# Low halves of split weights made by an accumulating DMA instead of VectorE, with a fourth weight tile pair, in a two-layer parallel-branch block

## The chip, the core and the metric

The kernel runs on one core of a Trainium2 chip. The metric is the device time of one execution in microseconds (us). The engines are TensorE (PE in the profile, with its weight loads shown as PEld), VectorE (DVE), ScalarE (ACT), GpSimd (POOL) and SyncE (SP), which here only issues DMA transfers. Each engine works through its own instructions in program order and waits on semaphores for the others.

## The reference, cut to what matters

Two layers act on a sequence x of 512 tokens and a context ctx of 256 tokens, both 1024 wide. In each layer a stream is normalised, scaled and shifted, and multiplied by a wide input matrix; four branches (retention, short convolution, a 31-tap convolution, attention) follow; each branch is multiplied by its own matrix and by a gate, and the sum goes through an output matrix.

```
hx = modulate(rmsnorm(x, norm_w[l]), shift_x, scale_x)
px = split_proj(hx @ w_in[l])               # q, k, v, gates of four branches
r, s, f, a = retention, short_conv, conformer_conv, windowed attention of px
merged = sum(sigmoid(g_i) * (br_i @ w_branch[i]) for i in range(4))
x = x + gate_x * (merged @ w_out[l])        # the context stream likewise in layer 0
```

All data are 32-bit floats.

## The kernel before

**Three products for one.** To keep 32-bit accuracy, each operand of a large matrix product is split in two float32r parts, a high part (the value copied to float32r) and a low part (the value minus its high part). The function `mm3` sums three products in PSUM: high weight by high data, high weight by low data, low weight by high data. A weight here is a block of 128 by 1024 numbers, eight 128 by 128 pieces, so one weight is 24 matmuls: of 512 columns for stream x, of 256 columns for the context.

**The path of a weight.** The list `wq` holds the weights in the order of their use. `w_load` takes the next one and issues its load on SP. A weight of stream x or of the output matrices of stream x is loaded whole (512 KB) into one of two raw tiles `w0`, `w1`. A weight of the context stream (its key ends in 1, called small below, since its product has 256 columns) is loaded in two halves of 256 KB into rows of the arena. `w_split` then makes the parts: ACT copies the raw data to the high tile `wh`, and DVE subtracts the high tile from the raw data into the low tile `wl` (lines 457 and 458). There are three pairs of tiles, `self.wt`, used in turn. `w_get` hands a weight to its matmuls, and `w_ahead(2)` splits until two weights beyond the one in use are ready. A gate weight ("g") brings along a block of 128 by 512 of a branch matrix, whose parts lie in arena rows; the change leaves those alone.

**What sets the order.** PE's instructions stand in the order in which the program is written. That order is made by `Tally`, a small planner: it adds up a cost for every instruction as it is issued, and `slot()` lets side work (attention, retention, the convolution, norms, written as generators) step forward between weights whenever the planner thinks that its inputs are ready and that DVE and ACT are not too far behind (`LEAD`, `LEADA`). Where side work waits for another engine's result, `settled()` adds `MARGIN`, 2 us, to the time at which the planner expects it. The other engines' orders are set by the framework's scheduler. Small powers of the norms run on POOL (`s_rs`, `s_rsr`, `s_lrs`).

**The stages.** Context of layer 0 (c0, small weights), stream x of layer 0 (x0), ten small weights for keys and values of the context in layer 1 (c1), stream x of layer 1 (x1). `final` computes the last output product in two halves of 256 columns, eight weights in the first half; three of them stay for the second half and five are loaded and split again.

All instructions are recorded through `call` of `Tallied`, so the profile puts nearly all of them on line 187; groups are told apart by tile names (`d`: PSUM of the large products; `k`: PSUM of side work; `p`: attention weights; `r`: arena rows).

Of the kernel before, what the change touches and what calls it, by code (L numbers as in the profile page):

```python
# [8 lines left out]
F32 = mybir.dt.float32  # L9
F32R = mybir.dt.float32r  # L10
BF16 = mybir.dt.bfloat16
AF = mybir.ActivationFunctionType
ALU = mybir.AluOpType
# [12 lines left out]
P = 128  # L26
# [97 lines left out]
class Row:  # L124
# [3 lines left out]
    def __init__(self, free, ring, tile, w, parts):  # L128
        self.free, self.ring = free, ring
        self.r = tile[:, :w] if parts else None  # L130
        self.a = tile[:, :w].bitcast(F32) if parts else tile[:, :w]
# [59 lines left out]
class Tally:  # L191
# [14 lines left out]
    def add(self, eng, op, a, k):  # L206
        aps = [x for x in (*a, *k.values()) if hasattr(x, "free_size")]
        out, src = aps[0], aps[1] if len(aps) > 1 else aps[0]
        n = src.free_size()
        ready = max([self.now, self.read.get(out.tensor.name, 0.0)] + [self.written.get(x.tensor.name, 0.0) for x in aps])  # L210
        if eng == "tensor":
            if op == "transpose":
                d = 0.109
            elif aps[2].dtype == F32:
                d = max(0.218, aps[2].free_size() / 600)
            else:
                d = aps[2].free_size() / 2400
                if aps[2].dtype == F32R and d < 0.1:
                    d = 0.213
            self.now += d  # L220
            end = self.now + 0.15
        else:
            if eng == "vector":
                d = 0.065 + n / 960
                if op in ("tensor_scalar", "tensor_copy") and n == src.free_size() and "PSUM" not in str(src.space):
                    d = 0.065 + n / 1920
            elif eng == "scalar":
                d = 0.1 + n / 1200
            elif eng == "gpsimd":
                d = 0.3 + n / 440  # L230
            else:
                d = 0.65
            start = max(self.busy[eng], ready)
            self.busy[eng] = max(self.busy[eng], self.now) + d
            end = start + d + 0.15
            if eng == "sync":
                end += 2.0 + n * out.shape[0] / 90000
        for x in aps:
            d = self.written if x is out or x is k.get("accum_out") else self.read
            d[x.tensor.name] = max(end, d.get(x.tensor.name, 0.0))  # L240
        self.last = max(self.last, end)
# [36 lines left out]
class Block:  # L278
    def __init__(self, ctx, tc, xc, vec, cst, w_a, w_g, w_b, w_o, w_m, out, out2):
        self.tc, self.nc = tc, Tally(tc.nc)  # L280
        self.xc, self.out, self.out2 = xc, out, out2
        self.wsrc = {"a": w_a, "g": w_g, "b": w_b, "o": w_o}
        self.w_m = w_m

        rp = ctx.enter_context(tc.tile_pool(name="rp", bufs=1))
        rp.tile([P, PAD], F32, name="fill")
        self.arena = Arena(rp, NROWS, 12)
        self.arena.relief = self.relief

        self.cp = cp = ctx.enter_context(tc.tile_pool(name="cp", bufs=1))  # L290
        self.wraw = [cp.tile([P, 1024], F32, name=f"w{i}") for i in range(2)]
        self.wt = [[cp.tile([P, 1024], F32R, name=f"w{p}{i}") for p in "hl"] for i in range(3)]
        self.pt = [cp.tile([P, 640], F32, name=f"p{i}") for i in range(6)]
        pp = ctx.enter_context(tc.tile_pool(name="pp", bufs=1, space=PSUM))
        nc = self.nc
        self.cst = cp.tile([P, NC_], F32, name="cst")
        self.vec = cp.tile([P, NV], F32, name="vec")
        nc.sync.dma_start(self.vec, vec)
        nc.sync.dma_start(self.cst[:, :NCE], cst[:, :NCE])
        self.late_consts = lambda: nc.sync.dma_start(self.cst[:, NCE:], cst[:, NCE:])  # L300
        self.rings = {}
        self.dense = [pp.tile([P, 512], F32, name=f"d{i}") for i in range(3)]
        self.ovs = [pp.tile([P, 512], F32, name="ov")]
        self.work = [pp.tile([P, 512], F32, name=f"k{i}") for i in range(4)]
        self.turn = {}
        self.wq, self.wraws, self.wready, self.wkeep = [], [], {}, {}
        self.lanes = [[] for _ in range(5)]
        self.turns = 0
        self.flow = None
# [115 lines left out]
    def w_load(self):  # L425
        key = self.wq.pop(0)
        kind, l, i, small = key
        nc = self.nc
        src = self.wsrc[kind][l, i]
        if small:  # L430
            raws = [(self.row(), slice(o, o + 512)) for o in (0, 512)]
            for r, o in raws:
                nc.sync.dma_start(r.a, src[:, o])
            raws = [(r, r.a, o) for r, o in raws]
        else:
            raw = self.take("wraw")
            nc.sync.dma_start(raw, src)
            raws = [(None, raw, slice(0, 1024))]
        if kind == "g":
            r = self.row()  # L440
            nc.sync.dma_start(r.a, self.wsrc["b"][l, i])
            raws.append((r, r.a, None))
        self.wraws.append((key, raws))

    def w_split(self):
        nc = self.nc
        key, raws = self.wraws.pop(0)
        parts = [self.take("wt")]
        for _, raw, o in raws:
            if o is None:  # L450
                hi, lo = self.part(), self.part()
                self.wkeep[key] = (hi, lo)
                hi, lo = hi.r, lo.r
                parts.append((hi, lo))
            else:
                hi, lo = (x[:, o] for x in parts[0])
            nc.scalar.activation(hi, raw, AF.Copy)
            nc.vector.tensor_tensor(lo, raw, hi.bitcast(F32), op=ALU.subtract)
        self.wready[key] = parts

    def w_ahead(self, n=2):
        while len(self.wready) < n and self.wraws:
            self.w_split()
        while self.wq and len(self.wraws) < (2 if self.wq[0][3] else 1):
            self.w_load()
# [1044 lines left out]
```

## Time and profile before

| quantity | value |
|---|---|
| median of 3 runs | 1831.37 us (1830.43 to 1831.96) |
| the profiled execution | 1828.66 us, of which the span from first to last instruction is 1826.9 us |
| granted TensorE clock, mean | 0.997 |
| busy share PE, PEld, DVE, ACT, POOL | 98%, 86%, 73%, 47%, 2% |
| DMA, all queues | 232.60 MB, mean 127 GB/s |

The span is what the trace shows; 1.8 us of the profiled execution lie around it. An engine's busy share is an average over stages that differ: what an engine's time is worth has to be read stage by stage, from what PE waits for there.

### The profile page before, as it was taken

To read this page: it belongs to the slowest core of one execution; us is meant where nothing else is said; L and a number is where in the kernel's file an instruction comes from. 1 tells how busy PE (TensorE), PEld (TensorE's weight loads), DVE (VectorE), ACT (ScalarE), POOL (GpSimd) and SP (SyncE) were. 2 spreads that over 40 slices of the span, in tenths; PEclk is the share of its full clock that TensorE was granted. 3 is DMA by queue.
4 is the path that set the end of the run, shared out by engine and by line. 5 is a ranking of instruction groups with operands and counts; after the bars stand their busy time and mean duration, and the time that the engine had idled before them with its cause. 6 is when DMAs were issued, how large, how long until landed. Compare 5 with 4: busy or idle time off the path is not lost. (4 is left out here: it accounts for less than half of the span.)

```text
span 1826.9 us, 27582 instructions
## 1 busy us (share of the span) xinstructions
PE 1798.4 (98%) x10242; PEld 1562.3 (86%) x10242; DVE 1326.9 (73%) x2635; ACT 851.6 (47%) x1625; POOL 27.9 (2%) x34
## 2 busy tenths in 40 slices
PE   6999999999999999999999999999999999999998
PEld 4999999988888888888888889888888888888888
DVE  8899999884556669996998457447999866344445
ACT  6666765553554544423423246445534554323223
POOL 1000000000000000000000000000000000000000
PEclk9999999999999999999999999999999999999999
DMA  9646477743222222233555552322222232332233
GB/s 315 246 129 207 120 239 231 233 138 116 70 70 68 83 81 80 95 113 124 183 167 170 159 190 76 116 70 70 65 92 84 84 95 91 111 105 90 87 116 116
DMA packets 104135, 232.60 MB, mean 127 GB/s; under 512 B 12864, under 2 KB 19776, under 8 KB 104000
## 3 DMA queue, kind: packets, MB, share of 16 engines
q1 hardware_dynamic: 104000, 230.84, 39.1%
q8 instruction: 80, 1.31, 0.3%
q14 instruction: 55, 0.45, 0.1%
HBM read 218.73 MB, written 5.24 MB: 123 GB/s over the span
## 5 line engine op out<-in xcount | busy, mean ns | idle before, releaser
L187 PE MATMUL d<-r,wh 128*128 128x512 f32 (+1 forms) x3136 | 942.8, 383 | 0.3 <-DVE r L187 0.3
L187 PEld LDWEIGHTS d<-r,wh 128*128 128x128 f32 x3136 | 572.7, 188 | 106.2 <-DVE r L187 0.8
L187 PE MATMUL d<-r,wl 128*128 128x512 f32 (+1 forms) x1568 | 597.6, 381 | 0.0
L187 DVE TENSOR_TENSOR wl<-w,wh 128x1024 fp32r<-128x1024 f32 x193 | 235.8, 1222 | 234.7 <-ACT wh L187 228.8
L187 ACT ACTIVATE wh<-w 128x1024 fp32r<-128x1024 f32 x193 | 204.9, 1062 | 412.0 <-PE d L187 354.8
L187 PEld LDWEIGHTS d<-r,wl 128*128 128x128 f32 x1568 | 294.8, 188 | 57.8
L187 ACT ACTIVATE r<-r 128x512 fp32r<-128x512 f32 (+3 forms) x264 | 150.6, 588 | 206.6 <-DVE r L187 93.8
L187 DVE TENSOR_TENSOR r<-r,r 128x512 fp32r<-128x512 f32 (+5 forms) x337 | 207.6, 630 | 33.4 <-ACT r L187 29.5
L187 DVE SCALAR_TENSOR_TENSOR r<-r,h_cfw,r 128x503 f32<-128x503 f32 (+19 forms) x360 | 229.4, 649 | 2.0
L187 PE MATMUL d<-r,r 128*128 128x512 f32 x768 | 184.8, 389 | 0.5 <-DVE r L187 0.5
L187 ACT ACTIVATE wh<-r 128x512 fp32r<-128x512 f32 x208 | 129.2, 630 | 101.7 <-PE d L187 90.0
L187 PEld LDWEIGHTS d<-r,r 128*128 128x128 f32 x768 | 144.1, 188 | 30.8 <-DVE r L187 0.9
L187 DVE TENSOR_TENSOR wl<-r,wh 128x512 fp32r<-128x512 f32 x208 | 140.6, 685 | 18.6 <-ACT wh L187 17.6
L187 DVE SCALAR_TENSOR_TENSOR r<-r,d 128x512 f32<-128x512 f32 (+1 forms) x156 | 92.8, 595 | 55.1 <-PE d L187 32.4
L187 ACT ACTIVATE r<-d 128x512 f32<-128x512 f32 (+2 forms) x234 | 118.5, 507 | 14.1 <-PE d L187 9.5
L187 PE MATMUL k<-r,r 128*128 128x128 f32 (+2 forms) x752 | 112.3, 290 | 2.7 <-ACT p L187 2.6
L187 ACT ACTIVATE r<-k 128x512 fp32r<-128x512 f32 (+4 forms) x162 | 77.0, 523 | 70.2 <-PE k L187 68.7
L187 PEld LDWEIGHTS k<-r,r 128*128 128x128 f32 x752 | 99.5, 191 | 9.0 <-ACT p L187 6.2
L187 ACT ACTIVATE p<-k,s_nm 128x256 f32<-128x256 f32 (+1 forms) x144 | 69.7, 496 | 77.0 <-DVE s_nm L187 76.8
L187 DVE SCALAR_TENSOR_TENSOR r<-r,cs,r 128x256 f32<-128x256 f32 x196 | 83.8, 480 | 1.0 <-DMA r<-w_m 0.4
L187 DVE TENSOR_TENSOR r<-k,r 128x512 fp32r<-128x512 f32 (+2 forms) x88 | 54.5, 653 | 9.2 <-ACT r L187 9.0
L187 ACT ACTIVATE p<-p,s_rc 128x512 f32<-128x512 f32 (+2 forms) x80 | 51.3, 719 | 8.6 <-DVE s_rc L187 8.6
(400 smaller groups left out, 2249.0 us busy)
## 6 DMA issues: line engine op xcount, KB each, us to landing
w<-w_a SPq DMA_DIRECT2D x108, 512.0 KB, 3.5
r<-w_a SPq DMA_DIRECT2D x128, 256.0 KB, 4.8
w<-w_g SPq DMA_DIRECT2D x64, 512.0 KB, 3.5
r<-w_m SPq DMA_DIRECT2D x96, 256.0 KB, 3.8
r<-w_b SPq DMA_DIRECT2D x96, 256.0 KB, 3.3
r<-w_g SPq DMA_DIRECT2D x64, 256.0 KB, 3.7
w<-w_o SPq DMA_DIRECT2D x21, 512.0 KB, 3.5
r<-xc SPq DMA_DIRECT2D x24, 256.0 KB, 3.9
```

The lines of the kernel that those rows point to most:

```text
L187: return f(*a, **k)
```

## The change

The low part of most weights is no longer made by DVE. ACT copies the high tile with factor -1 into the low tile, and a DMA that POOL issues then adds the weight, read once more from DRAM, to what stands there. This holds for every weight loaded whole after the third split, and for every other small weight (those whose running number is odd), there once for each half. There is a fourth pair of weight tiles, and `w_ahead` splits up to three weights ahead. The planner gets a cost for POOL's DMA, 1.0 us to issue and the landing time that it used for SP's.

```
             elif eng == "scalar":
                 d = 0.1 + n / 1200
+            elif eng == "gpsimd" and op == "dma_start":
+                d = 1.0
             elif eng == "gpsimd":
                 d = 0.3 + n / 440
...
-            if eng == "sync":
+            if op == "dma_start":
                 end += 2.0 + n * out.shape[0] / 90000
...
-        self.wt = [[cp.tile([P, 1024], F32R, name=f"w{p}{i}") for p in "hl"] for i in range(3)]
+        self.wt = [[cp.tile([P, 1024], F32R, name=f"w{p}{i}") for p in "hl"] for i in range(4)]
...
+        self.nsplit = 0
...
-            raws = [(r, r.a, o) for r, o in raws]
+            raws = [(r, r.a, o, src[:, o]) for r, o in raws]
         else:
             raw = self.take("wraw")
             nc.sync.dma_start(raw, src)
-            raws = [(None, raw, slice(0, 1024))]
+            raws = [(None, raw, slice(0, 1024), src)]
...
     def w_split(self):
         nc = self.nc
         key, raws = self.wraws.pop(0)
         parts = [self.take("wt")]
-        for _, raw, o in raws:
+        self.nsplit += 1
+        for _, raw, o, src in raws:
...
             nc.scalar.activation(hi, raw, AF.Copy)
-            nc.vector.tensor_tensor(lo, raw, hi.bitcast(F32), op=ALU.subtract)
+            if o and self.nsplit > 3 and (not key[3] or self.nsplit % 2):
+
+                nc.scalar.activation(lo, hi.bitcast(F32), AF.Copy, scale=-1.0)
+                nc.gpsimd.dma_start(lo, src, accum_op=ALU.add)
+            else:
+                nc.vector.tensor_tensor(lo, raw, hi.bitcast(F32), op=ALU.subtract)
         self.wready[key] = parts

-    def w_ahead(self, n=2):
+    def w_ahead(self, n=3):
```

In the built program 193 whole weights and 50 small ones go the new way. DVE loses 193 subtractions of 128x1024 and 100 of 128x512 (108 of that size stay), ACT gains as many copies `wl<-wh`, and POOL gains 293 DMA issues. PE has the same 9,700 rows of instructions in both programs; side work stands at other places among them.

DVE, in the attention of stream x, layer 1, where the largest scores (`s_mc`, `s_mx`) become the bias `s_nm` of the exponentials. Before:

```order
L187 TENSOR_REDUCE s_mx0_6125<-k0_160 128x1
L187 TENSOR_SCALAR s_ve3_2547<-s_mv3_2542 128x4
L187 TENSOR_REDUCE s_mx0_6125<-k1_161 128x1
L187 SCALAR_TENSOR_TENSOR r1414_13423<-r1361_12797,h_cfw1_763,r1414_13423 128x509
L187 TENSOR_TENSOR s_mc0_1876<-s_mc0_1876,s_mx0_6125 128x2
L187 TENSOR_TENSOR wl1_140<-w1_136,wh1_139 128x1024
L187 SCALAR_TENSOR_TENSOR s_nm0_1874<-s_mc0_1876,h_nsink1_769 128x2
L187 SCALAR_TENSOR_TENSOR r1414_13423<-r1361_12797,h_cfw1_763,r1414_13423 128x510
```

And with the change:

```order
L187 TENSOR_REDUCE s_mx0_6262<-k1_163 128x1
L187 TENSOR_REDUCE s_mx0_6262<-k2_164 128x1
L187 SCALAR_TENSOR_TENSOR r1390_13414<-r1361_13031,h_cfw1_765,r1390_13414 128x498
L187 TENSOR_TENSOR s_mc0_1939<-s_mc0_1939,s_mx0_6262 128x2
L187 SCALAR_TENSOR_TENSOR r1420_13773<-r1376_13247,h_cfw1_765,r1420_13773 128x503
L187 SCALAR_TENSOR_TENSOR s_nm0_1937<-s_mc0_1939,h_nsink1_771 128x2
L187 SCALAR_TENSOR_TENSOR r1390_13414<-r1361_13031,h_cfw1_765,r1390_13414 128x497
L187 SCALAR_TENSOR_TENSOR r1420_13773<-r1376_13247,h_cfw1_765,r1420_13773 128x504
```

Between the maximum `s_mc` and the bias `s_nm`, where the subtraction `wl` of a whole weight stood, a tap of the convolution stands now.

ACT, the same softmax: the copies of the splits and the exponentials `p`. Before:

```order
L187 ACTIVATE wh1_139<-w1_136 128x1024
L187 ACTIVATE r1419_13533<-d2_158 128x512
L187 ACTIVATE p4_147,s_ac0_1875<-k0_160,s_nm0_1874 128x256
L187 ACTIVATE p4_147,s_ac0_1875<-k3_163,s_nm0_1874 128x256
L187 ACTIVATE p5_148,s_ac0_1875<-k1_161,s_nm0_1874 128x256
L187 ACTIVATE p5_148,s_ac0_1875<-k3_163,s_nm0_1874 128x256
```

And with the change:

```order
L187 ACTIVATE wh0_137<-w0_135 128x1024
L187 ACTIVATE r1421_13788<-d2_160 128x512
L187 ACTIVATE wl0_138<-wh0_137 128x1024
L187 ACTIVATE p4_149,s_ac0_1938<-k1_163,s_nm0_1937 128x256
L187 ACTIVATE p4_149,s_ac0_1938<-k0_162,s_nm0_1937 128x256
L187 ACTIVATE p5_150,s_ac0_1938<-k2_164,s_nm0_1937 128x256
```

A second pass over the weight tile, `wl0<-wh0`, now stands between the evacuation of `d2` and the exponentials. Over all of ACT's program, 144 instructions are exponentials; 35 of them had a weight copy among the three instructions ahead before, 61 have one now.

POOL, the powers of the retention norms in stream x of layer 0. Before they stand alone:

```order
L187 TENSOR_TENSOR s_rs2_5837<-s_ms2_5836,cst_152 128x2
L187 TENSOR_TENSOR s_rsr0_1687<-s_ve0_1686,cst_152 128x4
L187 TENSOR_TENSOR s_rsr1_2014<-s_ve1_2013,cst_152 128x4
L187 TENSOR_TENSOR s_rsr2_2218<-s_ve2_2217,cst_152 128x4
L187 TENSOR_TENSOR s_rsr3_2548<-s_ve3_2547,cst_152 128x4
```

With the change the same power `s_rsr0` stands in one queue with the weights' DMA issues:

```order
L187 DMA wl0_138<-w_a 128x1024
L187 DMA wl1_140<-w_a 128x1024
L187 DMA wl2_142<-w_a 128x1024
L187 TENSOR_TENSOR s_rsr0_1728<-s_ve0_1727,cst_154 128x4
L187 DMA wl3_144<-w_a 128x1024
L187 DMA wl0_138<-w_a 128x1024
```

Each of these issues waits for ACT's copy into the same `wl` tile, and the power waits behind it in the queue.

## Rows read from the trace of the kernel before

**Rows 1.** The profile's page, its head and part 1: busy time by engine.

```profile
span 1826.9 us, 27582 instructions
PE 1798.4 (98%) x10242; PEld 1562.3 (86%) x10242; DVE 1326.9 (73%) x2635; ACT 851.6 (47%) x1625; POOL 27.9 (2%) x34
```

**Rows 2.** Busy time by stretch; PE, PEld, DVE, ACT, POOL, clock, DMA share, GB/s.

```profile
0.00:60.00 60.00, 44.48 (x297) 32.20 (x298) 51.17 (x171) 40.18 (x87) 4.91 (x7) 0.94 0.90 314
60.00:366.00 306.00, 306.00 (x2554) 305.26 (x2554) 282.80 (x674) 187.21 (x413) 6.36 (x7) 1.00 0.61 196
366.00:380.00 14.00, 13.43 (x107) 12.74 (x107) 12.77 (x22) 9.66 (x19) 0.00 (x0) 1.00 0.47 148
380.00:860.00 480.00, 478.14 (x2424) 402.17 (x2423) 343.50 (x634) 218.98 (x415) 7.46 (x9) 1.00 0.28 92
1105.00:1520.00 415.00, 412.28 (x2163) 348.03 (x2162) 314.37 (x589) 206.23 (x410) 6.57 (x8) 1.00 0.27 84
1772.00:1818.00 46.00, 45.88 (x382) 45.77 (x382) 27.41 (x50) 18.54 (x32) 0.70 (x1) 1.00 0.35 116
```

**Rows 3.** Waits of PE from 60 to 1818 us: total, times, longest.

```profile
PE k L187 <- ACT p L187: 3.4, 9, 0.7
PE d L187 <- DVE wl L187: 0.6, 1, 0.6
```

**Rows 4.** The chain that ended last, two pieces: start, us, what.

```profile
1524.31 244.86 PE d L187 x1080
1772.12 23.54 PE d L187 x194
```

**Rows 5.** The page's part 5, the groups that split weights.

```profile
L187 DVE TENSOR_TENSOR wl<-w,wh 128x1024 fp32r<-128x1024 f32 x193 | 235.8, 1222 | 234.7 <-ACT wh L187 228.8
L187 ACT ACTIVATE wh<-w 128x1024 fp32r<-128x1024 f32 x193 | 204.9, 1062 | 412.0 <-PE d L187 354.8
L187 ACT ACTIVATE wh<-r 128x512 fp32r<-128x512 f32 x208 | 129.2, 630 | 101.7 <-PE d L187 90.0
L187 DVE TENSOR_TENSOR wl<-r,wh 128x512 fp32r<-128x512 f32 x208 | 140.6, 685 | 18.6 <-ACT wh L187 17.6
```

**Rows 6.** Order of time near 1375 us, in x1: start, us, instruction.

```profile
1373.04 1.01 POOL L187 TENSOR_TENSOR s_rsr<-s_ve,cst 128x4 f32<-128x4 f32 x1 [35.22 <-DVE s_ve L187]
1373.79 0.15 DVE L187 TENSOR_TENSOR s_mc<-s_mc,s_mx 128x2 f32<-128x2 f32 x1
1373.86 1.22 DVE L187 TENSOR_TENSOR wl<-w,wh 128x1024 fp32r<-128x1024 f32 x1
1375.00 0.15 DVE L187 SCALAR_TENSOR_TENSOR s_nm<-s_mc,h_nsink 128x2 f32<-128x2 f32 x1
1375.11 0.33 SPq L187 DMA_DIRECT2D w<-w_a  x1
1377.23 0.39 PE L187 MATMUL k<-r,r 128*128 128x256 f32 x1 [0.67 <-ACT p L187]
```

**Rows 7.** Order of time near 95 us, ACT's halves of a small weight.

```profile
95.03 0.63 ACT L187 ACTIVATE wh<-r 128x512 fp32r<-128x512 f32 x1 [0.54 <-PE d L187]
96.47 0.63 ACT L187 ACTIVATE wh<-r 128x512 fp32r<-128x512 f32 x1 [0.81 <-PE d L187]
```

**Rows 8.** The page's part 6, weight loads: KB each, us to landing.

```profile
r<-w_a SPq DMA_DIRECT2D x128, 256.0 KB, 4.8
w<-w_o SPq DMA_DIRECT2D x21, 512.0 KB, 3.5
```

**Rows 9.** Order of time in the final stage, ACT.

```profile
1778.56 1.06 ACT L187 ACTIVATE wh<-w 128x1024 fp32r<-128x1024 f32 x1 [1.74 <-DMA w<-w_o]
1779.53 0.40 ACT L187 ACTIVATE r<-r 128x256 f32<-128x256 f32 x1
```

**Rows 10.** Waits of ACT and of DVE, the longest of each.

```profile
ACT wh L187 <- PE d L187: 444.7, 235, 6.6
...
DVE wl L187 <- ACT wh L187: 246.5, 125, 4.9
```

## The prediction on record

> **What bounds the kernel now.** The head of the page and its busy times come first: PE is busy for 1798.4 of 1826.9 us, DVE for 73% and ACT for 47% [rows 1]. A busy PE need not be at its peak, so the chain that ended last is next. In its two long pieces PE runs one matmul of 512 columns per 244.86 / 1080 = 0.227 us and one of 256 columns per 23.54 / 194 = 0.121 us, with nothing between them [rows 4]. A weight's 24 matmuls so take 5.44 us in stream x and 2.91 us where the product has 256 columns. The change leaves every one of them in place, so what it can win is only time in which PE has nothing to do. The table by stretch shows how little that is: 60 - 44.48 = 15.5 us in the first 60 us, and afterwards 0.57, 1.86 and 2.72 us in the three stretches that show any to speak of, 5.2 us together; in the context stage from 60 to 366 us there is none, though DVE is busy there for 282.8 of 306 us, 92% [rows 2]. The last view is that of PE's own waits after 60 us: 3.4 us for ACT's attention weights `p`, in nine waits, and one wait of 0.6 us for a low part that DVE made late [rows 3]. A DVE that is nearly full thus costs this kernel almost nothing by itself; it costs something where a softmax stands behind it.
>
> **The change, part by part.**
>
> *DVE gives up subtractions.* 193 of 1.222 us and 100 of 0.685 us are 235.8 + 68.5 = 304 us of its 1326.9 [rows 1, 5]. It also stops standing at the head of its queue for ACT's high part, 246.5 us in 125 waits [rows 10]. What of this reaches PE is seen near 1375 us: the maximum is there at 1373.94, a subtraction of 1.22 us runs in front of the bias `s_nm`, the exponentials follow, and PE waits 0.67 us for them [rows 6]. Without the subtraction that wait goes. The program before has a subtraction of a whole weight at most five DVE instructions ahead of `s_nm` in 13 of the 32 softmaxes' halves of the x streams; the program with the change has none. The gain lies between 0 and the 5.2 us of idle time; I take half, 2.6 us, since about half of the places are of this kind.
>
> *ACT takes copies.* 193 of 1.062 us (the size of `wh<-w`) and 100 of 0.630 us are 205 + 63 = 268 us, which brings it to 1120 us, 61% [rows 1, 5]. Sums hide this; the queue does not. 35 exponentials had a weight copy among the three instructions ahead, 61 will, and each such copy is up to 1.06 us in front of the `p` that PE waits for. Scaled by that, the 3.4 us of [rows 3] become 3.4 x 61 / 35 = 5.9 us, 2.5 us more. The planner counts the new copies, however, and moves the transposes behind them, so the cost lies between 0 and 2.5 us and I take 1.3. It pulls at the same waits as the gain on DVE.
>
> *POOL takes 293 DMA issues.* The trace has none on POOL. An issue on SP takes 0.33 us, a power on POOL 1.01 us [rows 6]; I take 1.0, the row of the same engine. That is about 300 us spread over the span on an engine that is busy 28 us [rows 1].
>
> *The landing of an accumulating transfer* is the number that matters and that no row shows. The lower bound is a plain load of the same size: 3.5 us for 512 KB, 4.8 us for 256 KB in the busy context stage [rows 8]. The upper bound is twice that, 7.0 and 9.6 us, should reading the old contents cost as much again as reading the weight. I take 5 and 6.5 us, nearer to the plain load, since part of a landing is not data.
>
> Whether it is hidden follows from the time between a tile's release and its next use, which is three weights with the fourth pair.
> - Stream x: 3 x 5.44 = 16.3 us at least. Needed: two copies 2.1, issue 1.0, landing 7.0 at worst, 10.1 us. Hidden with 6 us to spare, so nothing is added.
> - Final stage: 3 x 2.91 = 8.7 us. Needed before landing: two copies, the square of 0.40 us between them [rows 9], the issue, 3.5 us; 5.2 us are left. At 5 us this fits; at 7.0 us each of some eight weights is 1.8 us late, and since a delay of one weight also gives time to the next two, this costs 1.8 / 3 x 8 = 4.8 us.
> - Context: ACT's two halves of a small weight follow each other by 96.47 - 95.03 = 1.44 us, half a weight, each waiting for PE [rows 7]; the first half is thus free half a weight early and has 3.5 x 2.91 = 10.2 us. Two copies of 0.63 and the issue take 2.3, so 7.9 us are left for the landing. At 6.5 us it fits; at 9.6 us it is 1.7 us late, for some 25 of the input weights.
>
> I add 0 for late landings.
>
> *DMA load.* From 60 to 366 us the engines are 0.61 busy at 196 GB/s, so full is about 321 GB/s [rows 2]. Some 39 small weights add 20 MB there, 67 GB/s: 0.21 if a byte is paid once, 0.42 if twice, 0.82 or 1.03 in all. In stream x, 0.28 at 92 GB/s leaves room either way.
>
> The Trainium skill, DMA: Bandwidth & Descriptors, section Anatomy of one DMA — SWDGE (gpsimd) path, gives a fit of 2.0 us plus the bytes at 436 GB/s for a DMA issued by GpSimd, by which 512 KB would land in an estimated 3.2 us and 256 KB in 2.6 us. By that the late landings would be 0 at either bound; the loads of [rows 8] take 3.5 and 4.8 us in this kernel, and the sum goes by those.
>
> *The first three splits* keep the old way, and the 15.5 us of idle time at the start and the end of the span stay. The powers on POOL now wait behind issues that wait for ACT; the planner's margin of 2 us (`MARGIN`) hides the usual case, and I add nothing.
>
> *Sum:* -2.6 + 1.3 + 0 = -1.3 us. The profiled execution took 1828.66 us (span 1826.9), 2.7 us less than the median of 1831.37; on the scale of the runs the forecast is 1831.37 - 1.3 = 1830 us.
>
> **The rivals.** A change within 0.2% (3.7 us) can hardly be told from none; the cases are cut there.
> - *Faster, 1826.5 us.* ACT never stands in the way and DVE's relief returns nearly all of the 5.2 us of idle time, 4.9. For it: DVE's queue loses the work and the 246.5 us of standing. Against it: the waits of [rows 3] name ACT, which becomes fuller. The bound is 5.2 us, so no more than 0.3%.
> - *Slower, late landings, 1840 us.* Past 7.9 us of landing in the context stage PE waits for low parts: at 8.5 us, 0.6 us late, two thirds of it lasting for each of 25 weights is 10 us, less the 1.3 of the sum. For it: the load above comes near 1, and 4.8 us is already the plain landing. Against it: side work lengthens the period beyond 2.91 us. At 9.6 us it would be 1.7 x 0.67 x 25 = 28 us.
> - *Slower, queues of ACT and POOL, 1837 us.* ACT's 2.5 us come in full, and eight retention powers of the x streams wait about a microsecond each behind DMA issues, with half of that reaching PE: 6.5 us less a gain of 1. For it: ACT already waits 444.7 us for PE with a weight copy at the head of its queue [rows 10], 1.9 us each, and everything behind it on POOL now waits too.
> - *Slower, POOL held up by DVE, 1837 us.* With DVE 92% busy in the context stage [rows 2], an issue that had to wait for three DVE instructions of 0.685 us [rows 5] would come 2 us later; 6.5 + 2 passes the 7.9 us by 0.6 us, which for two thirds of the 25 weights is 0.6 x 0.67 x 17 = 7 us, less 1.3. The Trainium skill, SBUF — State Buffer, section Who interferes with whom, states such a lock for GpSimd's descriptors, against DVE instructions in a two-port mode. No row here shows POOL and DVE at odds.
>
> **How the numbers follow.** Chances: the forecast (no change that can be measured) 0.40, faster 0.30, late landings 0.15, ACT and POOL 0.11, POOL held up 0.04. That gives faster 0.30, same 0.40, slower 0.30. The range from 1824.5 to 1841 us reaches below the faster case by 2 us, since ends of matmuls are modelled and gaps too small to be shown as idle are not in the 5.2 us, and up to late landings of 0.6 us; beyond it lie heavier ones. The forecast's own range is 1827.7 to 1835.
>
> **What the profile of the changed kernel would show.** DVE near 1023 us busy and ACT near 1120. A landing time of POOL's transfers in the page's part on DMA issues: under 7.9 us for 256 KB and 5.2 us for 512 KB if I am right. PE's waits for `p` of much the same sum, and none for a DMA into `wl`. The prediction fails if PE waits for `wl` by DMA anywhere between 60 and 366 us or after 1772 us, or if the DMA share from 60 to 366 us comes near 1.

## The result and the profile after

The changed kernel takes 1882.55 us (median of 4 runs, 1878.54 to 1884.01), the kernel before 1831.13 us beside it. The ratio is 1.0277 (95% interval 1.0259 to 1.0295): 51 us slower, far beyond the range of the prediction. The profiled execution took 1883.28 us.

The page of the changed kernel: its span, busy times, the two DMA queues (packets, MB, share of 16 engines' time), and landing times.

```profile
span 1881.5 us, 28151 instructions
PE 1819.4 (97%) x10242; PEld 1577.2 (84%) x10242; DVE 1053.5 (56%) x2342; ACT 1082.7 (58%) x1918; POOL 281.4 (15%) x327
...
q0 software_dynamic: 42192, 127.42, 40.1%
q1 hardware_dynamic: 104000, 230.84, 36.7%
...
w<-w_a SPq DMA_DIRECT2D x108, 512.0 KB, 3.9
wl<-w_a POOLq DMA_DIRECT2D x108, 512.0 KB, 6.5
r<-w_a SPq DMA_DIRECT2D x128, 256.0 KB, 5.8
...
r<-w_b SPq DMA_DIRECT2D x96, 256.0 KB, 5.0
```

The new queue q0 moves 127 MB and takes more of the engines' time than the plain 231 MB: 40.1 / 127.42 = 0.315% for a MB against 36.7 / 230.84 = 0.159%. An accumulated byte takes 1.98 times what a plain one takes. A plain load of 256 KB now lands in 5.8 us where it was 4.8 [rows 8].

Busy time by stretch (columns as in [rows 2]; the last stretch is the final stage, 46 us later than before):

```profile
0.00:60.00 60.00, 44.35 (x276) 31.57 (x276) 49.89 (x176) 42.32 (x92) 8.54 (x11) 0.86 0.92 319
60.00:366.00 306.00, 290.60 (x2366) 288.00 (x2367) 227.59 (x556) 215.11 (x466) 70.64 (x82) 0.98 0.93 245
380.00:860.00 480.00, 468.44 (x2447) 397.36 (x2447) 273.54 (x576) 288.70 (x500) 67.03 (x78) 0.99 0.71 163
1105.00:1520.00 415.00, 409.95 (x2181) 348.04 (x2180) 240.27 (x497) 256.56 (x457) 62.01 (x70) 1.00 0.73 165
1818.00:1870.00 52.00, 48.40 (x383) 47.40 (x382) 18.18 (x42) 26.80 (x41) 9.21 (x11) 0.97 0.83 200
```

DVE is relieved everywhere, from 282.8 to 227.6 us in the context stage [rows 2], and yet PE now stands in every stretch. The DMA share rose from 0.61 to 0.93 there and from 0.28 to about 0.72 in stream x. The waits of PE from 45 us on (total, times, longest), where before 3.4 us for `p` were all there was to speak of [rows 3]:

```profile
PE k L187 <- ACT p L187: 11.7, 13, 3.5
PE d L187 <- DMA wl<-w_a: 9.2, 5, 4.0
PE d L187 <- ACT r L187: 8.1, 4, 3.3
PE d L187 <- DMA wl<-w_o: 3.7, 4, 2.2
PE d L187 <- DVE r L187: 3.4, 4, 2.6
```

Of these 12.9 us are for late low parts. The rest is ACT and DVE being late. The waits for `p` among them hardly belong to the transfers: the two longest, 3.5 us at 737.63 and 2.8 at 778.18, are 3.1 and 2.4 us at the same two matmuls in the run of experiment 3 that has no low parts to make. In ACT's own list of waits the largest for a DMA is that for the rows of the branch matrices (`w_b`). Before:

```profile
ACT r L187 <- DMA r<-w_b: 49.7, 19, 5.1
```

and after:

```profile
ACT r L187 <- DMA r<-w_b: 147.1, 37, 10.4
```

How such a stand travels is read in order of time, in the context stage of the changed kernel (SP's queue, ACT, DVE, POOL and PE):

```profile
195.28 0.33 SPq L187 DMA_DIRECT2D r<-w_b  x1
...
205.21 0.63 ACT L187 ACTIVATE r<-r 128x512 fp32r<-128x512 f32 x1 [8.02 <-DMA r<-w_b]
...
206.40 0.69 DVE L187 TENSOR_TENSOR wl<-r,wh 128x512 fp32r<-128x512 f32 x1 [7.85 <-ACT wh L187]
...
207.32 0.63 ACT L187 ACTIVATE wl<-wh 128x512 fp32r<-128x512 f32 x1
...
208.24 0.86 POOL L187 DMA_DIRECT2D wl<-w_a  x1 [10.76 <-ACT wl L187]
...
209.16 0.36 PE L187 MATMUL d<-r51h,wh 128*128 128x256 f32 x1 [1.48 <-ACT wl L187]
...
211.47 0.48 ACT L187 ACTIVATE p<-k,s_nm 128x256 f32<-128x256 f32 x1 [1.03 <-DVE s_nm L187]
...
214.28 0.39 PE L187 MATMUL d<-r51h,wl 128*128 128x256 f32 x1 [1.78 <-DMA wl<-w_a]
```

A row of `w_b` is issued at 195.28 and ACT, which works in order, stands at it for 8.02 us. Behind it on ACT are the next weight's copies. DVE stands 7.85 us for one of them, with the softmax's bias behind it, so the exponentials come later too. POOL's next accumulating transfer starts after 10.76 us of standing, with about 6 us of landing still to come, and PE stands 1.48 us for ACT and 1.78 us for that low part.

Not every stand of PE has this origin. In the changed kernel 6.5 us of PE's waits, from 209 to 331 us, come right behind a stand of ACT at `w_b`. Another 8.3 us, at 353, 395, 400 and 1092 us, come behind a stand of ACT or DVE at rows of the streams themselves, loaded from DRAM (`xc`, `xd`); the longest such stand is 8.01 us. Waits for low parts of 0.8 and 4.0 us are at the first accumulated weights, where ACT didn't stand at a load:

```profile
57.10 0.87 POOL L187 DMA_DIRECT2D wl<-w_a  x1 [2.53 <-PE d L187]
...
63.69 0.39 PE L187 MATMUL d<-r109h,wl 128*128 128x256 f32 x1 [4.05 <-DMA wl<-w_a]
```

PE came to this low part at 59.6, only 2.5 us after its transfer was issued.

The trace's DMA view from 180 to 220 us shows why the `w_b` row was late: each digit is the busy share of 1 us, and the loads take 7 to 10 us.

```profile
DMA  9999999999999999999999991000666999726688
...
r<-w_a SPq DMA_DIRECT2D x9, 256.0 KB, 9.9
...
r<-w_b SPq DMA_DIRECT2D x4, 256.0 KB, 7.4
```

A stand costs more than its length. Stretches of 4 us in the changed kernel's stream x, with the granted clock behind POOL's count:

```profile
730.00:734.00 4.00, 4.00 (x19) 3.08 (x17) 3.94 (x9) 2.12 (x2) 0.33 (x1) 1.00 0.27 62
734.00:738.00 4.00, 0.50 (x2) 0.29 (x1) 4.00 (x10) 2.15 (x8) 0.53 (x1) 0.90 0.84 184
738.00:742.00 4.00, 4.00 (x16) 3.39 (x16) 2.99 (x7) 0.00 (x0) 0.00 (x0) 0.50 0.21 41
742.00:746.00 4.00, 4.00 (x15) 3.16 (x14) 3.96 (x10) 1.04 (x2) 0.00 (x0) 0.74 0.00 0
```

PE stands for 3.5 us, and the 4 us that follow are granted 0.50, the level of 1.2 GHz. (This stand is the first of the two for `p` named above, but the transfers' stands are followed by such stretches as well: 0.60 from 64 to 68 us, 0.70 from 216 to 220.) Over the span, the same 10242 matmuls are busy for 1819.4 - 1798.4 = 21.0 us more [rows 1]. The mean granted clock fell from 0.997 to 0.986. The share that is missing to 1, times the span, is 5.5 us before and 26.3 us after; by this estimate nearly all of the 21 us are such slow matmuls. The other 33.6 of the 54.6 us of longer span are idle time.

### The profile page after: what moved, and what is told of

Read it like the earlier page. It is cut to its first block, busy times and chain, and to the rows that moved or that the text cites. A ratio compares the mean times of both kernels' runs of the same rounds, so it can differ in the third digit from the quotient of the medians.

```text
span 1881.5 us, 28151 instructions
## 1 busy us (share of the span) xinstructions
PE 1819.4 (97%) x10242; PEld 1577.2 (84%) x10242; DVE 1053.5 (56%) x2342; ACT 1082.7 (58%) x1918; POOL 281.4 (15%) x327
## 3 DMA queue, kind: packets, MB, share of 16 engines
q0 software_dynamic: 42192, 127.42, 40.1%
q1 hardware_dynamic: 104000, 230.84, 36.7%
## 4 chain that ended last, share of the span: by engine, by line
PE 74%; DMA 8%; DVE 8%; issue 7%; ACT 3%; POOL 1%; SPq 0%; POOLq 0%; DVEq 0%; ACTq 0%
PE d L187 64%; PE k L187 9%; DVE r L187 6%; PE ov L187 2%; DMA r<-w_o 1%; DMA r<-w_m 1%; ACT p L187 1%; DMA r<-xc 1%; DMA wl<-w_a 1%; DMA r<-w_b 1%; DMA wl<-w_o 1%; ACT wh L187 1%; DMA w<-w_a 1%; ACT r L187 1%; POOL wl L187 1%
## 5 line engine op out<-in xcount | busy, mean ns | idle before, releaser
L187 ACT ACTIVATE r<-r 128x512 fp32r<-128x512 f32 (+3 forms) x264 | 150.0, 588 | 280.6 <-DMA r<-w_b 147.1
L187 ACT ACTIVATE wl<-wh 128x1024 fp32r<-128x1024 f32 (+1 forms) x293 | 265.9, 908 | 2.8
L187 POOL DMA_DIRECT2D wl<-w_a x168 | 146.5, 872 | 792.0 <-ACT wl L187 651.1
L187 DVE SCALAR_TENSOR_TENSOR r<-r,h_cfw,r 128x509 f32<-128x509 f32 (+25 forms) x360 | 227.1, 652 | 4.2
L187 POOL DMA_DIRECT2D wl<-w_g x96 | 83.0, 874 | 575.5 <-ACT wl L187 378.6
L187 DVE TENSOR_TENSOR wl<-r,wh 128x512 fp32r<-128x512 f32 x108 | 73.4, 687 | 40.6 <-ACT wh L187 38.5
```

The costliest lines, as they stand in the source:

```text
L187: return f(*a, **k)
```

## Experiments

All times are medians, with the ratio to the kernel before as it ran on the same chip. In the diffs `nc.add` only tells the planner of an instruction, and `nc.nc` issues one that the planner isn't told of; so the order can be held while the work is changed. In the traces TensorE's 10242 instructions stand in the changed kernel's order, or in that of the kernel before, in every run but "whole weights alone"; the orders of DVE and ACT shift somewhat with the work. "The 293 pieces" are the 193 whole weights and 100 halves that the change treats.

**1. The new order with the old work, and with ACT's copies.** In `w_split` of the changed kernel; first run:

```
-                nc.scalar.activation(lo, hi.bitcast(F32), AF.Copy, scale=-1.0)
-                nc.gpsimd.dma_start(lo, src, accum_op=ALU.add)
+                nc.add("scalar", "activation", (lo, hi, AF.Copy), {})
+                nc.add("gpsimd", "dma_start", (lo, src), {})
+                nc.nc.vector.tensor_tensor(lo, raw, hi.bitcast(F32), op=ALU.subtract)
```

> The changed kernel's order of instructions on TensorE, its four pairs of tiles and its three weights ahead, but DVE makes every low part by a subtraction again; no negated copies on ACT and no accumulating transfers. If the loss of 51 us is in the transfers (bytes paid about twice, loads late) or in ACT's extra copies, this gives 1826 to 1845 us (some loss may stay, since the order counts on a DVE without subtractions). If the loss is in the order and the longer lookahead themselves, it gives more than 1865 us.

Measured: 1876.63 us, 1.0248 (1.0233 to 1.0263). In the second run the copy on ACT stays, and DVE adds the raw weight to it.

> The order of the changed kernel with its 293 negated copies on ACT, but DVE adds the raw weight to the copy where the accumulating transfer did it. If ACT's fuller queue is the cause, this keeps most of the loss: more than 1860 us, with ACT near 1080 us busy. If the transfers are the cause, 1830 to 1850 us.

Measured: 1880.34 us, 1.0269 (1.0253 to 1.0284). Neither run has a single accumulating transfer, and both are slow, with PE waiting 28 us for `p`. By the expectations they would put the loss on the order and on ACT's queue, which doesn't follow: they tell that ACT's copies add little (4 us), but not whether the order is slow by itself, since DVE's subtractions stand in an order that doesn't count on them. Run 3 separates that.

**2. The transfers alone, beside the kernel before.** The kernel before keeps its subtractions; a copy of one column makes POOL wait for the weight's high part, then the transfer goes into a tile that nobody reads:

```
+            if o and self.nsplit > 3 and (not key[3] or self.nsplit % 2):
+                s = self.scr[self.nsplit // (2 if key[3] else 1) % 2][:, o]
+                g = nc.nc.gpsimd
+                g.tensor_copy(s[:, :1], hi.bitcast(F32)[:, :1])
+                g.dma_start(s, src, accum_op=ALU.add)
```

> The kernel before with its three pairs and its subtractions, and beside that the same 293 accumulating transfers from POOL, at the time of the same weights, into two scratch tiles that nobody reads. If an accumulating byte takes the time of about two plain bytes and the other loads come late for it, this alone gives 1850 to 1885 us, with a DMA share above 0.9 from 60 to 366 us and the w_b loads at about 5 us instead of 3.3. If the loss needs late low parts or ACT's copies, it stays within 4 us of 1831 us.

The others have one edit each: no `accum_op`; half of the columns; 16 columns.

> As the run with transfers into scratch tiles, but plain transfers that don't accumulate, so the same issues and the same bytes from DRAM. If accumulating costs a byte twice, the share of q0 in the DMA engines' time falls from about 40 to about 20 percent and the time is 1832 to 1848 us, clearly below the accumulating version. If POOL's queue (powers behind issues) costs the time, it is as slow as the accumulating version.

> The kernel before with the 293 accumulating transfers into scratch tiles, of half the columns each: as many issues on POOL, half the bytes. If the loss goes by the time that the transfers take of the DMA engines, this is that of the plain transfers of all columns (q0 about 20 percent, 1836 to 1846 us). If it comes from accumulating as such, or from the number of transfers, it stays near 1876 us.

> The kernel before with the 293 transfers into scratch tiles cut to 16 columns: POOL has the same small copies and the same issues to make, and next to no bytes move. If the 8 to 9 us that remain with plain transfers or with half the columns come from the DMA engines, this is within 4 us of the kernel before. If they come from POOL's queue, it is 1836 to 1843 us as well.

Measured: accumulating 1875.88 us, 1.0243 (1.0224 to 1.0262); plain 1840.33 us, 1.0053 (1.0035 to 1.0071); accumulating half the columns 1838.34 us, 1.0046 (1.0031 to 1.0061); 16 columns 1832.29 us, 1.0008 (0.9999 to 1.0017). The line of POOL's queue on the pages, accumulating in full:

```profile
q0 software_dynamic: 42192, 127.42, 39.1%
```

plain:

```profile
q0 software_dynamic: 35792, 127.42, 19.4%
```

half the columns:

```profile
q0 software_dynamic: 42192, 63.72, 21.7%
```

The same bytes take 39.1% accumulating and 19.4% plain, so accumulating a byte takes the engines' time twice over, and the loss goes by that time, not by accumulating as such or by the bytes: plain in full and accumulating half the columns differ in bytes by a factor of two and cost the same within 1 us. It doesn't go in proportion: about 20% of the engines' time costs 8 to 9 us, 39% costs 45. POOL's queue with all its issues costs about 2 us, no more than the interval can tell from nothing.

In stream x of the accumulating version, order of time:

```profile
747.19 0.33 SPq L187 DMA_DIRECT2D r<-w_b  x1
...
754.42 0.63 ACT L187 ACTIVATE r<-r 128x512 fp32r<-128x512 f32 x1 [6.11 <-DMA r<-w_b]
...
755.57 0.69 DVE L187 SCALAR_TENSOR_TENSOR r<-r,d 128x512 f32<-128x512 f32 x1 [4.93 <-ACT r L187]
756.17 0.15 DVE L187 SCALAR_TENSOR_TENSOR s_nm<-s_mc,h_nsink 128x2 f32<-128x2 f32 x1
...
756.38 0.46 ACT L187 ACTIVATE p<-k,s_nm 128x256 f32<-128x256 f32 x1
...
761.28 0.33 PE L187 MATMUL k<-cst,p 128*128 128x128 f32 x1 [2.75 <-ACT p L187]
```

ACT stands 6.11 us at a `w_b` row, DVE 4.93 us at ACT, the softmax's bias stands behind DVE's instruction, and PE stands for `p`. No low part is late here. The load's landing is off PE's path until a queue stands at it in which work of the path is behind.

**3. The ladder in the new order.** The changed kernel with the work taken out: first neither copies nor transfers (the first four lines of the diff of run 1), then the copies alone, then transfers of half the columns.

> The order of the changed kernel with its four pairs and three weights ahead, and the low parts of the 293 pieces not made at all (this leaves out their part of the result: the products read old low parts). DVE, ACT and the transfers are all without the work in question. If the order and the longer lookahead cost time of their own, this stays above 1860 us, as the run of the order with DVE's subtractions did (1876.6). If that run was slow only because the order counts on a DVE without subtractions, it gives 1820 to 1832 us, and the softmax stands of 4 to 7 us near 711 and 1447 us are gone.

> The order of the changed kernel with its 293 negated copies on ACT, but no accumulating transfers and no subtractions (this leaves out the weight in these low parts, which hold the negated high part). One step above the run of the order alone (1838.8 us). If ACT's copies cost what the prediction allowed for them, 0 to 2.5 us, this is 1837 to 1843 us, and all the rest up to 1882 us belongs to the transfers. If ACT's queue is the cause, it is above 1855 us.

> The changed kernel, each accumulating transfer over half of its columns only (the other half of the low part keeps the negated high part, so this leaves out half of the sums): every copy, issue and wait is kept, the transfers take half the DMA engines' time. If the loss goes by that time and falls off once the engines have room, as it did beside the kernel before (+45 us with all columns, +8 with half), this is 1843 to 1856 us. If the waits and the queues of ACT and POOL as such cost the time, it stays above 1865 us.

Measured: 1838.81 us, 1.0049 (1.0034 to 1.0064); 1840.56 us, 1.0055 (1.0041 to 1.0069); 1852.14 us, 1.0121 (1.0107 to 1.0134). Against 1830.3 us of the kernel before, measured beside them, the steps are: order 8.5, copies 1.7, half of the transfers' columns 11.6, the other half 30.4 us (1882.55 less 1852.14, measured at another time). The order, with its fourth pair and third weight ahead, which no run takes apart, is slow even with nothing to do for DVE, less than the 30 us that I had put against it, and more than the gain that I had hoped for. Where it loses is seen in the run without low parts, order of time:

```profile
699.65 0.66 PE L187 MATMUL k<-r,r 128*128 128x384 f32 x3
...
702.95 0.74 DVE L187 SCALAR_TENSOR_TENSOR r<-r,h_cfw,r 128x502 f32<-128x502 f32 x1
703.61 0.68 DVE L187 TENSOR_REDUCE s_mc<-k 128x2 f32<-128x512 f32 x1
...
706.46 0.15 DVE L187 SCALAR_TENSOR_TENSOR s_nm<-s_mc,h_nsink 128x2 f32<-128x2 f32 x1
...
708.84 0.44 PE L187 MATMUL k<-r,r 128*128 128x384 f32 x1 [3.09 <-ACT p L187]
```

The scores are done at 700.3. DVE comes to their maximum at 703.61, because taps of the 31-tap convolution (`r<-r,h_cfw,r`) stand in front of it: DVE's freed time, which the planner counts on, went to side work ahead of the softmax that PE waits for. PE stands 3.09 us here and 2.37 at 747.59, and 7.9 us for `p` after 60 us, where it was 3.4 before. That the rest of the 8.5 us, mostly longer matmuls, follows from these stands is not shown by a run of its own.

The run with the copies alone has the same order of PE as the changed kernel and not one transfer, so the two can be set beside each other matmul by matmul. The changed kernel's span is 44.2 us longer: 17.6 us in longer matmuls (1819.4 against 1801.8) and 26.5 us in waits. From 45 us on PE waits 27.3 us more: 12.9 for low parts that land late, 13.5 for what ACT and DVE made late, 13.0 of it right behind their stands at `w_b`, `xc` and `xd`, and under 1 us for `p`.

**4. Which stage, and which load.** The first run accumulates whole weights alone; the second issues the `w_b` row ahead of its weight; the third does that in the kernel before:

```
-            if o and self.nsplit > 3 and (not key[3] or self.nsplit % 2):
+            if o and self.nsplit > 3 and not key[3]:
```

```
         src = self.wsrc[kind][l, i]
+        if kind == "g":
+            rb = self.row()
+            nc.sync.dma_start(rb.a, self.wsrc["b"][l, i])
         if small:
```

> The changed kernel with accumulating transfers for whole weights alone (193, streams x and the last stage); in the context stages DVE subtracts. If the loss sits where the DMA engines come near full (60 to 366 us with a share of 0.93), most of it goes: 1840 to 1855 us, with about 18 us less from 60 to 500 us, and the part of stream x left. If the loss comes from the order in stream x or from POOL and ACT there, it stays above 1865 us.

> The changed kernel, but the load of the branch matrix's row (w_b) is issued ahead of the loads of its weight (w_g) and not behind them. If ACT standing at late w_b rows (147 us in 37 waits) is what carries the late loads to TensorE, the w_b waits fall by more than half and the time falls by 10 us or more, to under 1873 us. If all loads are late together and TensorE waits for others just as much, it stays within 5 us of 1882 us.

> The kernel before with the load of the branch matrix's row issued ahead of its weight's loads. In the changed kernel this gave back 7 us of the 51. In the kernel before ACT stands 50 us in 19 waits for these rows, but TensorE has only 5 us of idle time after the first 60 us: if some of that comes from these waits, 1826 to 1830 us; if not, within 3 us of 1831. A loss of a few us at the start, where the engines are 0.9 busy, is possible too.

Measured: whole weights alone 1862.93 us, 1.0178 (1.0163 to 1.0193); `w_b` first 1875.59 us, 1.0246 (1.0222 to 1.0271), with 129.7 us of ACT's waits for `w_b` left of 147.1; in the kernel before 1830.74 us, 1.0000 (0.9991 to 1.0009). The first misses both expectations: 33 of the 51 us are there with whole weights alone (an order's share among them, of unknown size: the planner, told of other work, made an order of its own), in stages where the engines' share is only about 0.7. The second lies between its two: an earlier issue gives back some 7 us, by medians measured at different times and with intervals that overlap, but the row still lands late among the others. ACT's waits for `w_b` are a poor measure of the loss: they are 78.7 us without low parts and with plain transfers, which cost 9 us each, and 91.6 us for the change in the old order (run 5), which costs 45.

**5. The old order: DVE's relief alone, and the change's work.** From the kernel before; the first leaves out the 293 subtractions (the planner is still told of them), the second puts the copies, the transfers and the fourth pair in their place, two weights ahead as before:

```
+                nc.add("vector", "tensor_tensor", (lo, raw, hi.bitcast(F32)), {})
+                nc.nc.scalar.activation(lo, hi.bitcast(F32), AF.Copy, scale=-1.0)
+                nc.nc.gpsimd.dma_start(lo, src, accum_op=ALU.add)
```

> The kernel before in its own order, with the same 293 subtractions left out and nothing in their place (this leaves out these low parts). It measures the gain from DVE's relief alone, which the prediction took as 2.6 us out of at most 5.2. If the relief is worth that, 1826 to 1829 us; if TensorE's waits for the softmax don't come from the subtractions, within 1.5 us of the kernel before; below 1825 us would mean that idle time is not all that DVE costs.

> The changed kernel's copies on ACT, accumulating transfers and four pairs of tiles, but in the order of the kernel before and two weights ahead: only the planner's new order is taken away. If order and transfers cost time apart from each other (8.5 and some 42 us), this is 1866 to 1878 us, near the run with transfers into scratch tiles (1875.9) less DVE's relief. If low parts that land late for want of the third weight ahead cost more than the order, it is above 1885 us.

Measured: 1826.73 us, 0.9981 (0.9972 to 0.9990), which is 3.2 us less; and 1875.32 us, 1.0239 (1.0224 to 1.0255). The relief is worth 3 us, 2 to 5 by the interval; the transfers cost about as much in either order.

**6. The change only where a softmax is near.** As the last, for 14 weights of 297:

```
+            if o and self.nsplit in NEAR:
```

> The order of the kernel before with four pairs of tiles, and the change's copies and accumulating transfers for 14 whole weights alone: those whose subtraction stands at most six DVE instructions ahead of a softmax's bias in stream x. DVE's relief is kept where it counts, and 7 of the 127 MB are moved. If the relief is worth 3 us mostly at these places and the transfers' cost goes by their bytes (some 45 x 7.3 / 127 = 2.6 us at most), this is 1827 to 1830 us. If ACT's extra copies ahead of the exponentials take the gain back, it is within 1.5 us of the kernel before; above 1834 us a single transfer at a softmax costs more than its share.

Measured: 1829.39 us, 0.9994 (0.9985 to 1.0003), no difference from the kernel before. Whether copies and transfers use up a gain here, or the relief at these 14 places gives none, no run separates; no version that does all of the work beats the kernel before.

**Where each lost its time.** Worked out from the traces: the start of the n-th matmul into `d` less that of the n-th in the trace of before, in us. Each comes from one profiled execution, so a difference of 2 or 3 means nothing.

```
at (time before)          60   366   500   700   860  1180  1770  1815
changed                  7.4  25.7  31.0  24.1  42.4  47.6  48.8  53.8
no low parts, new order  1.8   3.2   2.7  -4.3  11.7   9.8   9.1   9.1
into scratch, old order  0.4  10.7  16.7  16.7  23.0  34.5  40.9  46.8
change in old order      7.2  23.5  29.2  28.6  29.3  40.9  43.5  48.5
whole weights alone      1.4   1.4   7.1   6.4  20.9  27.7  29.7  34.3
```

Half of the loss arises by 366 us, the rest in bursts: around 400, at the attention of layer 0 (the order's share), at the start of stream x of layer 1, and in the final stage. The scratch version and the change in the old order agree in their total, but not in the places: the first loses 11 us by 366 us against 24, and more in stream x. Late low parts do cost something in the context stage.

## Why the prediction was wrong

The step that failed is the term for late landings, put at 0 because the DMA engines seemed to have room and the new landings seemed hidden. The accumulating transfers cost 42 us, and neither reason held. Step by step:

- *The bound.* Right: PE had 5.2 us to win. DVE's relief, taken as 2.6 us, measured 3.2; ACT's copies, taken as 1.3, measured 1.7 (run 3). POOL's issue, taken as 1.0 us, is 0.87, and its queue costs about 2 us. None of these is the cause. DVE's and ACT's busy times, 1053.5 and 1082.7 us, came out near the 1023 and 1120 forecast. No sign shows of issues held up by DVE either. The view of the tile `wl` (ns: least, median, greatest) shows it for the issues that read `w_a`; none of the 293 is above 1.24 us:

```profile
L187 POOL DMA_DIRECT2D wl<-w_a x168: 862/862/1231, 51.0 to 1524.4; - x168
```

- *"I take 5 and 6.5 us, nearer to the plain load".* The second value held (256 KB took 6.3 us from `w_a`, 6.7 from `w_g`), the first was too low: for 512 KB it is 6.5 us, near the upper bound of 7.0, and 8.1 for `w_o`. That an accumulated byte costs as much again is what the engines' time shows (39.1 against 19.4%); that reading the old contents is the reason is not shown. The fit that the Trainium skill gives in DMA: Bandwidth & Descriptors, section Anatomy of one DMA — SWDGE (gpsimd) path, 3.2 us by estimate, does not hold for accumulating transfers here.
- *"Hidden with 6 us to spare", "I add 0 for late landings".* The criterion was wrong more than the number. In the context stage 256 KB of `w_a` landed in 6.3 us in the median, within the 7.9 us (8 of 76 transfers there took longer), and PE still waited 6.7 us for `wl` up to 366 us, in three waits. At the first accumulated weights the lead that I counted on was not there yet (2.5 us in place of 7.9, 4.9 us lost). At 214 us the time was lost ahead of the issue, while ACT stood at `w_b` (1.8 us). I counted how long the new transfer takes, but not how late it makes the old ones, and those cost as much of PE's waits again (13.0 beside 12.9 us).
- *"In stream x, 0.28 at 92 GB/s leaves room either way".* It cost about as much as the context stage: in the table above, the changed kernel less the run without low parts loses 22.5 us by 366 us and 22.2 behind it. Whole weights alone lose 33 us at a share of 0.65 to 0.84; were their order to cost the 8.5 us of the changed kernel's, 24 of them would be the transfers', an estimate. The views to weigh were the page's landing times and ACT's waits for DMA: 49.7 us for `w_b` already stood in the trace of before, next to the row that I did use [rows 10].
- *"The first three splits keep the old way, and the 15.5 us ... stay".* They did, but some 7 us more were lost right behind them, at the first accumulated weights, at 57 to 64 us, in the change in either order and with half the columns too, but not with the transfers into scratch tiles or for whole weights alone.
- *"The planner counts the new copies, however".* True, but it also counts DVE as free, and side work fills it ahead of the softmax: 8.5 us for the new order that the prediction had nowhere.
- *The rivals.* Late landings named the right direction at a fifth of the size and only one of its places. What failed was the range's reach: its upper end came from 0.6 us of late landing in one stage. The signs named for failure, PE waiting for `wl` by DMA and a share near 1, both came true.

The steps of the ladder, 8.5, 1.7 and 42.0 us, add up by construction to 52.2 us, which is 1882.55 less 1830.3. From outside, the run with the transfers beside the kernel before shows that such transfers can cost as much, 44.5 us, without the new order, the copies or a low part that depends on them, though at other places. In the changed kernel what the transfers add to PE's waits divides about evenly between late low parts and what other late loads hold up. How the whole 42 us, slower matmuls included, would divide is not settled: a version of the change in which only the low parts are late was not run.

## What to carry to other kernels

Before moving work to the DMA engines, price it in the engines' time and not in bytes, and then ask which in-order queue stands at another load that will land later, and what of the critical path is behind it; an average share of 0.7 did not mean room here. Ask also what a planner does with the time it is told is free: here side work came to stand ahead of the softmax. And when an engine is 73% busy but the one that bounds waits 5 us in all, its relief is worth at most those 5 us, and everything the relief costs elsewhere is set against them.

## What the hardware showed beyond this

- An accumulating transfer takes twice the DMA engines' time of a plain one of the same bytes (39.1 and 19.4% of the span, transfers into scratch tiles), and its issue on POOL 0.87 us against 0.54.
- In this kernel the loss grows faster than the load: +20% of the engines' time cost 8 to 9 us, +39% cost 45.
- After a stand of 3.5 us PE ran at the level of 1.2 GHz (granted 0.50) for 4 us and more; 21 us of the longer span are longer matmuls and not waiting.
